# Split input weights kept in DRAM for later token tiles, and element work moved from GpSimd to VectorE

## The chip, the core and the metric

One core of one Trainium2 chip. The metric is the device time of one execution in microseconds (us); the lower, the better. Engines in the profile: PE is TensorE's matmul and PEld its weight load, DVE is VectorE, ACT is ScalarE, POOL is GpSimd, SP is SyncE, which here issues the DMAs.

## What is computed

One layer of a hybrid decoder block on x of 2048 tokens by 1024 features. `u = RMSNorm(x)`, then one projection `z = u @ W_in` whose columns feed two groups of heads: four mLSTM heads (columns for q, k, v, output gate and two gate columns per head) and four heads of differential attention (q, k, v). Both groups' outputs go through `W_out` and are added to x. After that come an MLP (`W_down (relu(norm @ W_up))^2`) and a gated per-layer embedding. All of it is float32 in the reference.

## The kernel before, in words

**Precision.** A float32 operand is split into two parts, hi and lo, and each product is three matmuls: hi by hi, hi by lo, lo by hi (`mm3`, lines 134 to 139; the three matmuls are lines 137, 138 and 139). The split itself is `split` (lines 74 to 76): ScalarE copies raw to hi (L75), and GpSimd, unless VectorE is named, subtracts hi from raw to give lo (L76).

**Two phases.** `phase1` (lines 176 to 594) makes the projection, both head groups and the first half of the output projection. `phase2` (from line 849) does the MLP and the rest; the change does not touch its code.

**Phase 1's projection.** The tokens are four tiles of 512 (j = 0 to 3). For each tile there is an attention pass ("a", 6 groups of 256 or 264 weight columns) and an mLSTM pass ("m", 8 groups of 256 columns), in the order a0, a1, a2, m0, m1, a3, m2, m3 (`ORDER`, line 37). So there are 4 times 14 = 56 group uses of 14 different groups. `load_w` (lines 242 to 256) loads one group as four pieces of 128 x 512 (128 x 528 for the group with the gate columns): a DMA from `w_in` into one of two raw buffers (L248), then `split` into one of eight slots of `wbuf`. `next_w` (line 265) is called when a group begins, and loads one group ahead of the one in use. As each group is used once per token tile, all 56 uses load and split their weights anew: 224 DMAs, 222 copies on ScalarE and 222 subtractions on GpSimd (two pieces of the very first group are split on VectorE alone, L251 and L252).

**The inputs.** `make_u` (line 313) runs at each change of token tile, eight times in all. `u_front` (lines 270 to 299) loads 128 tokens of x (L286), and the first time that a tile is seen it squares them on ScalarE (L291) and sums the eight feature blocks by three halving additions (L295), on VectorE for tile 0 and on GpSimd for the others; then VectorE multiplies by the norm's gain (L298). `u_back` (line 301) splits the result into hi and lo, the subtraction on VectorE, but on GpSimd for the odd blocks of tiles 1 to 3 (12 times in all), and makes the token's scale by a matmul with ones (L308) and a power on GpSimd (L310).

**Attention beside it.** `attention` (line 432) is a second generator that a credit counter interleaves with the projection (lines 572 to 593); it works on 64 units of 128 queries by one head. `attn_front` makes scores (L786, L789), their row maximum on VectorE (L790), the exponential on ScalarE (L798), and the difference of the two maps on VectorE (L810). `attn_back` transposes (L822), multiplies by V (L834), copies out (L837), makes the norm's factor (L840 to L842 and a power on GpSimd, L843) and scales the output by it on GpSimd (L844); a transposition on TensorE (L500) takes it from there. `qk_prep` (line 723) norms and rotates q and k on VectorE (L733, L736, L742 to L751) with a power on GpSimd between (L734), and `k_out` transposes them on TensorE (L758). `mlstm` runs one head's chunks in steps between the matmuls. The order of the instructions on each engine is set at build time by a scheduler that simulates the timeline, so it need not be that of the text.

Of the kernel before, what the change touches and what calls it, by code (L numbers as in the profile page):

```python
# [7 lines left out]
F32 = mybir.dt.float32  # L8
F32R = mybir.dt.float32r
BF16 = mybir.dt.bfloat16  # L10
AF = mybir.ActivationFunctionType
ALU = mybir.AluOpType
AX = mybir.AxisListType
# [3 lines left out]
P = 128  # L17
D = 1024
S = 2048
KT = D // P  # L20
# [19 lines left out]
@with_exitstack  # L40
def hybrid_block(ctx: ExitStack, tc: tile.TileContext, a: dict, out: bass.AP):
    nc = tc.nc

    const = ctx.enter_context(tc.tile_pool(name="const", bufs=1))
    dram = ctx.enter_context(tc.tile_pool(name="dram", bufs=1, space=DRAM))

    shared = ctx.enter_context(tc.tile_pool(name="shared", bufs=1))
    banks = Banks(ctx.enter_context(tc.tile_pool(name="banks", bufs=1, space=PSUM)))

    yT = [dram.tile([D, T2], F32, name=f"yT_d{i}") for i in range(NT2)]  # L50
    hd = dram.tile([D, T1], F32, name="h_d")
    qkdr = dram.tile([NH, NT1, P, 4, T1], F32, name="qk_d")
    vdr = dram.tile([NH // 2, NT1, P, 4, 2 * P], F32, name="v_d")

    wbuf = shared.tile([P, 2 * NW * 528], F32R, name="wbuf")
    ubuf = shared.tile([P, 16 * T1], F32R, name="ubuf")
    ybuf = shared.tile([P, 3 * 1024], F32R, name="ybuf")
    pre = shared.tile([P, T1], F32, name="pre")
    acc0 = shared.tile([P, T1], F32, name="acc0")
    rbuf = shared.tile([P, max(4096, 3072 + NR * 528)], F32, name="rbuf")  # L60

    ident = const.tile([P, P], F32, name="ident")
    identr = const.tile([P, P], F32R, name="identr")
    identb = const.tile([P, P], BF16, name="identb")
    masks = const.tile([P, 2, P], BF16, name="masksb")
    ones = const.tile([P, P], F32, name="ones")
    nc.vector.memset(ones, 1.0)
    negh = const.tile([P, 1], F32, name="negh")
    g23 = const.tile([P, 3, KT], F32, name="g23")
    nc.vector.memset(negh, -0.5)  # L70
    warm = const.tile([P, 1], F32, name="warm")
    nc.scalar.activation(warm, negh, AF.Copy)

    def split(raw, hi, lo, eng=nc.gpsimd):
        nc.scalar.activation(hi, raw, AF.Copy)  # L75
        eng.tensor_tensor(out=lo, in0=raw, in1=hi.bitcast(F32), op=ALU.subtract)  # L76

    nb = T1 // P

    def rstd_col(sq, pc, v):  # L80

        for b in range(nb):
            nc.tensor.matmul(pc[:, b:b + 1], lhsT=sq[:, b * P:(b + 1) * P], rhs=ones[:, 0:1], start=True, stop=True)
        nc.vector.tensor_scalar(out=v, in0=pc[:, 0:nb], scalar1=1.0 / D, scalar2=EPS, op0=ALU.mult, op1=ALU.add)
        nc.gpsimd.tensor_tensor(out=v, in0=v, in1=negh.broadcast_to([P, nb]), op=ALU.pow)

    def spread(v, pb, out_t):

        for b in range(nb):
            nc.vector.tensor_scalar(out=out_t[:, b * P:(b + 1) * P], in0=ident, scalar1=v[:, b:b + 1], scalar2=None,  # L90
                                    op0=ALU.mult)
        nc.tensor.matmul(pb, lhsT=ones, rhs=out_t, start=True, stop=True)
        nc.vector.tensor_copy(out_t, pb)

    phase1(tc, a, wbuf, ubuf, rbuf, banks, yT, hd, qkdr, vdr, ident, identr, identb, masks, ones, negh, split, rstd_col, spread, acc0)
    phase2(tc, a, wbuf, ubuf, rbuf, ybuf, pre, acc0, g23, banks, yT, hd, out, split, rstd_col, spread)


def cut(buf, base, *dims, cast=None):
    n = 1  # L100
    for d in dims:
        n *= d
    t = buf[:, base:base + n]
    if cast:
        t = t.bitcast(cast)
    if len(dims) == 2:
        t = t.rearrange("p (a b) -> p a b", a=dims[0])
    elif len(dims) == 3:
        t = t.rearrange("p (a b c) -> p a b c", a=dims[0], b=dims[1])
    return t  # L110
# [62 lines left out]
        return cut(t[0:shape[0]], 0, *shape[1:], cast=None if dtype == F32 else dtype)  # L173


def phase1(tc, a, wbuf, ubuf, rbuf, ps, yT, hd, qkdr, vdr, ident, identr, identb, masks, ones, negh, split, rstd_col, spread, acc0):
    nc = tc.nc
    with ExitStack() as ctx:
        pool = lambda name, bufs=1, **k: ctx.enter_context(tc.tile_pool(name=name, bufs=bufs, **k))
# [3 lines left out]
        pm = Ring(pool("p1m"))  # L183
        pc = pool("p1c")
        pw = Ring(None)
        half = NW * 528
        for tag, base in (("whi", 0), ("wlo", half)):
            pw.put(tag, [cut(wbuf, base + i * 528, 2, 264) for i in range(NW)])
        pu.put("xk", [cut(rbuf, i * 1024, KT, P) for i in range(2)])
        pu.put("sq", [cut(rbuf, 2048, KT, P)])  # L190
        pw.put("wraw", [cut(rbuf, 3072 + i * 528, 2, 264) for i in range(NR)])
# [47 lines left out]
        gB = gcol.unsqueeze(2).broadcast_to([P, KT, P])  # L239
        pl = lambda t: t.rearrange("p a b -> p (a b)")  # L240

        def load_w(g, width, first=False):
            r = []
            for k in range(0, KT, 2):
                raw = pw.tile([P, 2, 264], F32, tag="wraw")[:, :, :width]
                hi = pw.tile([P, 2, 264], F32R, tag="whi")
                lo = pw.tile([P, 2, 264], F32R, tag="wlo")
                nc.sync.dma_start(raw, w_in[g, :, k:k + 2, :width])  # L248
                hi, lo = hi[:, :, :width], lo[:, :, :width]
                if first and k % 4 == 0:  # L250
                    nc.vector.tensor_copy(hi, raw)  # L251
                    nc.vector.tensor_tensor(out=lo, in0=raw, in1=hi.bitcast(F32), op=ALU.subtract)  # L252
                else:
                    split(raw, hi, lo)
                r += [(hi[:, i], lo[:, i]) for i in range(2)]
            return r

        wseq, wq = [], []
        for kind, j in ORDER:
            if kind == "a":  # L260
                wseq += [(8, 264)] + [(8 + g, 256) for g in range(1, 6)]
            else:
                wseq += [(g, 256) for g in (0, 1, 2, 3, 4, 5, 7, 6)]

        def next_w():
            while wseq and len(wq) < 1 + AHEAD:
# [3 lines left out]
        def u_front(j, tb):  # L270
            if rcol[j] is None:
                rcol[j] = pc.tile([P, 2, 4], F32, name=f"rcol{j}")
                stats.add(j)
            xk = pu.tile([P, KT, P], F32, tag="xk", name="xk")
            start = j == 0 and tb == 0 and j in stats
            if start:
                for k in range(KT):
                    if k % 4 == 0:
                        nc.sync.dma_start(xk[:, k:k + 4], a["x_in"][0, :, k:k + 4])
                    if k == 0:  # L280
                        wq.append(load_w(*wseq.pop(0), True))
                    nc.scalar.activation(Uh[:, 0, k], xk[:, k], AF.Copy, scale=gcol[:, k:k + 1])
                    nc.vector.scalar_tensor_tensor(out=Ul[:, 0, k], in0=xk[:, k], scalar=gcol[:, k:k + 1],
                                                   in1=Uh[:, 0, k].bitcast(F32), op0=ALU.mult, op1=ALU.subtract)
            else:
                nc.sync.dma_start(xk, a["x_in"][4 * j + tb])  # L286
            acc = None
            if j in stats:
                sq = pu.tile([P, KT, P], F32, tag="sq", name="sq", bufs=1)
                acc = pu.tile([P, P], F32, tag="acc", name="acc", bufs=2)  # L290
                nc.scalar.activation(pl(sq), pl(xk), AF.Square)  # L291
                n = KT // 2
                while n:
                    o = sq[:, 0:n] if n > 1 else acc.unsqueeze(1)
                    (nc.gpsimd if j > 0 else nc.vector).tensor_tensor(out=o, in0=sq[:, 0:n], in1=sq[:, n:2 * n], op=ALU.add)  # L295
                    n //= 2
            if not start:
                nc.vector.tensor_tensor(out=xk, in0=xk, in1=gB, op=ALU.mult)  # L298
            return None if start else xk, acc

        def u_back(j, tb, xk, acc):
            if xk is not None:
                split(xk, Uh[:, tb], Ul[:, tb], nc.gpsimd if j and tb % 2 else nc.vector)
            if acc is not None:
                r = rcol[j]
                c = r[:, 0, tb:tb + 1]
                pr = ps.tile([P, 1], F32, "m")
                nc.tensor.matmul(pr, lhsT=acc, rhs=ones[:, 0:1], start=True, stop=True)  # L308
                nc.vector.tensor_scalar(out=c, in0=pr, scalar1=1.0 / D, scalar2=EPS, op0=ALU.mult, op1=ALU.add)
                nc.gpsimd.tensor_tensor(out=c, in0=c, in1=negh, op=ALU.pow)  # L310
                nc.vector.tensor_scalar(out=r[:, 1, tb:tb + 1], in0=c, scalar1=0.5, scalar2=None, op0=ALU.mult)
# [503 lines left out]
def attn_back(nc, pa, ps, st, i, h, front, VV, ident, negh, out):  # L815
# [25 lines left out]
    nc.vector.scalar_tensor_tensor(out=ss[:, 1:2], in0=ll[:, 0:1], scalar=EPS, in1=ll[:, 0:1], op0=ALU.mult, op1=ALU.mult)  # L841
    nc.vector.scalar_tensor_tensor(out=ss[:, 0:1], in0=ss[:, 0:1], scalar=1.0 / P, in1=ss[:, 1:2], op0=ALU.mult, op1=ALU.add)  # L842
    nc.gpsimd.tensor_tensor(out=ss[:, 0:1], in0=ss[:, 0:1], in1=negh, op=ALU.pow)  # L843
    nc.gpsimd.tensor_scalar(out=y, in0=y, scalar1=ss[:, 0:1], scalar2=None, op0=ALU.mult)  # L844
    out.append(y)
    yield 0.5

# [375 lines left out]
```

## Time and profile before

| | us |
|---|---|
| median of three runs | 3005.1 (3004.28 to 3007.91) |
| the profiled execution, its own time | 2999.47 |
| its span, first to last instruction | 2997.7 |
| TensorE matmul busy in the span | 2872.7 (96%) |
| VectorE, ScalarE, GpSimd busy | 1963.7, 1377.7, 1267.0 |
| mean granted TensorE clock | 0.988 |

Busy time is the union of an engine's instructions. A wait is put down to whoever released it last. Phase 1 fills the span up to some 1290 us and phase 2 the rest; the eight projection passes begin at about 6 (a0), 112 (a1), 242 (a2), 372 (m0), 525 (m1), 703 (a3), 839 (m2) and 1016 us (m3), and m3's last group ends at about 1220 us.

### The profile page before, as it was taken

How to read it: one execution, taken by the hardware profiler on the slowest of the kernel's cores; microseconds unless marked ns; L12 is line 12 of the kernel's file. 1: busy time of each engine (PE TensorE's matmuls, PEld its weight loads, DVE VectorE, ACT ScalarE, POOL GpSimd, SP SyncE). 2: the span in 40 equal slices, each digit the busy share in tenths (PEclk: the TensorE clock that was granted, in tenths of full speed). 3: DMA queues.
4: the chain of work that ended last, by engine and by line, in shares of the span. 5: the costliest groups of instructions: out<-in, count | busy, mean ns of one | idle time of the engine just before them, and what ended most of it. 6: DMA issues, size and time to landing. Idle time of an engine off the chain costs nothing.

```text
span 2997.7 us, 43151 instructions
## 1 busy us (share of the span) xinstructions
PE 2872.7 (96%) x15752; PEld 2460.7 (82%) x15752; DVE 1963.7 (66%) x3917; ACT 1377.7 (46%) x3134; POOL 1267.0 (42%) x980
## 2 busy tenths in 40 slices
PE   7798999899999899989999999999999999999999
PEld 7787988888988788867888888888878888888887
DVE  7788777767786766567555656564486555565653
ACT  4476766766666665544223332252342233322331
POOL 5666543434443332344333333362563333333441
PEclk9899999999999999999999999999999999999999
DMA  5654544334443423341111111124411111111211
GB/s 160 193 159 146 175 135 123 110 103 138 140 128 96 123 81 100 105 163 49 51 57 43 57 57 50 53 75 154 134 60 53 57 43 57 57 50 50 80 48 64
DMA packets 202421, 282.57 MB, mean 94 GB/s; under 512 B 16096, under 2 KB 143584, under 8 KB 198112
## 3 DMA queue, kind: packets, MB, share of 16 engines
q1 hardware_dynamic: 202208, 279.81, 30.7%
q8 instruction: 124, 2.03, 0.3%
q14 instruction: 89, 0.73, 0.1%
HBM read 239.90 MB, written 39.85 MB: 93 GB/s over the span
## 4 chain that ended last, share of the span: by engine, by line
PE 69%; DVE 14%; ACT 5%; DMA 4%; issue 4%; POOL 3%; SPq 0%; POOLq 0%; ACTq 0%; DVEq 0%
PE bank L923 52%; PE bank L137 3%; PE bank L138 3%; PE bank L139 3%; PE bank L834 2%; DMA rbuf<-in_w_in_dram 2%; DVE qn_r L736 2%; POOL wbuf L76 2%; DVE PP_r L810 2%; ACT PP_r L798 1%; DVE mxp_r L790 1%; PE bank L786 1%; PE bank L789 1%; PE bank L822 1%; POOL rn_r L734 1%
## 5 line engine op out<-in xcount | busy, mean ns | idle before, releaser
L76 POOL TENSOR_TENSOR wbuf<-rbuf,wbuf 128x512 fp32r<-128x512 f32 (+2 forms) x632 | 911.8, 1450 | 1321.8 <-ACT wbuf L75 1230.0
L75 ACT ACTIVATE wbuf<-rbuf 128x512 fp32r<-128x512 f32 (+2 forms) x632 | 415.1, 662 | 870.2 <-PE bank L923 600.7
L923 PE MATMUL bank<-U_r,wbuf 128*128 128x512 f32 x2928 | 701.1, 392 | 10.3 <-POOL wbuf L76 4.7
L923 PEld LDWEIGHTS bank<-U_r,wbuf 128*128 128x128 f32 x2928 | 551.1, 189 | 129.9 <-POOL wbuf L76 6.1
L923 PE MATMUL bank<-ubuf,wbuf 128*128 128x512 f32 x2208 | 574.7, 391 | 2.2 <-DVE ubuf L76 1.4
L888 DVE TENSOR_TENSOR h_r<-bank,h_r 128x512 f32<-128x512 f32 x504 | 343.3, 688 | 269.1 <-PE bank L923 267.5
L923 PEld LDWEIGHTS bank<-ubuf,wbuf 128*128 128x128 f32 x2208 | 414.8, 188 | 92.7 <-issue 2.9
L923 PE MATMUL bank<-ybuf,wbuf 128*128 128x512 f32 x1872 | 477.5, 390 | 5.4 <-ACT wbuf L75 4.6
L923 PEld LDWEIGHTS bank<-ybuf,wbuf 128*128 128x128 f32 x1872 | 351.3, 188 | 80.2 <-ACT wbuf L75 5.9
L137 PE MATMUL bank<-wbuf,ubuf 128*128 128x256 f32 (+1 forms) x1280 | 381.1, 298 | 25.0 <-ACT og_r L397 10.1
L138 PE MATMUL bank<-wbuf,ubuf 128*128 128x256 f32 (+1 forms) x1280 | 375.4, 293 | 0.9 <-DVE wbuf L252 0.9
L139 PE MATMUL bank<-wbuf,ubuf 128*128 128x256 f32 (+1 forms) x1280 | 373.6, 292 | 0.6 <-DVE ubuf L76 0.6
L137 PEld LDWEIGHTS bank<-wbuf,ubuf 128*128 128x128 f32 x1280 | 250.4, 196 | 34.1 <-ACT og_r L397 12.6
L138 PEld LDWEIGHTS bank<-wbuf,ubuf 128*128 128x128 f32 x1280 | 251.1, 196 | 3.9 <-DVE wbuf L252 1.5
L139 PEld LDWEIGHTS bank<-wbuf,ubuf 128*128 128x128 f32 x1280 | 250.5, 196 | 2.8 <-DVE ubuf L76 0.7
L790 DVE TENSOR_REDUCE mxp_r<-bank 128x1 f32<-128x512 f32 (+3 forms) x320 | 186.3, 603 | 68.6 <-PE bank L789 68.1
L798 ACT ACTIVATE PP_r<-bank,mx_r 128x512 f32<-128x512 f32 (+3 forms) x320 | 196.3, 622 | 53.8 <-DVE mx_r L795 47.4
L834 PE MATMUL bank<-V_r,at_r 128*128 128x128 f32 x1088 | 137.8, 279 | 0.9 <-ACT at_r L825 0.5
L786 PE MATMUL bank<-KT_r,QT_r 128*128 128x512 f32 (+3 forms) x320 | 124.7, 390 | 12.8 <-ACT PP_r L798 10.9
L834 PEld LDWEIGHTS bank<-V_r,at_r 128*128 128x128 f32 x1088 | 132.3, 196 | 3.4 <-ACT at_r L825 0.8
L137 PE MATMUL bank<-ubuf,wbuf 128*128 128x512 f32 x320 | 130.2, 407 | 2.4 <-DVE mx_r L794 1.2
L139 PE MATMUL bank<-ubuf,wbuf 128*128 128x512 f32 x320 | 127.8, 399 | 0.0
(285 smaller groups left out, 4244.8 us busy)
## 6 DMA issues: line engine op xcount, KB each, us to landing
rbuf<-in_w_in_dram SPq DMA_DIRECT2D x208, 256.0 KB, 2.8
rbuf<-in_w_down_dram SPq DMA_DIRECT2D x128, 256.0 KB, 2.6
rbuf<-in_w_up_dram SPq DMA_DIRECT2D x32, 1024.0 KB, 4.8
KT_r<-qk_d SPq DMA_DIRECT2D x40, 512.0 KB, 5.0
qk_d<-kst_r SPq DMA_DIRECT2D x64, 256.0 KB, 3.1
QT_r<-qk_d SPq DMA_DIRECT2D x128, 128.0 KB, 3.4
rbuf<-in_w_out_dram SPq DMA_DIRECT2D x32, 512.0 KB, 3.8
rbuf<-in_x_in_dram SPq DMA_DIRECT2D x31, 512.0 KB, 3.8
```

What stands on the lines that cost most here:

```text
L75: nc.scalar.activation(hi, raw, AF.Copy)
L76: eng.tensor_tensor(out=lo, in0=raw, in1=hi.bitcast(F32), op=ALU.subtract)
L137: nc.tensor.matmul(ps, lhsT=lh, rhs=rh, start=(start and i == 0), stop=False)
L138: nc.tensor.matmul(ps, lhsT=lh, rhs=rl, start=False, stop=False)
L139: nc.tensor.matmul(ps, lhsT=ll, rhs=rh, start=False, stop=(stop and i == n - 1))
L736: nc.vector.scalar_tensor_tensor(out=qn[:, e], in0=qn[:, e], scalar=rn[:, e:e + 1], in1=qkg[:, e // 2], op0=ALU.mult, op1=ALU.mult)
L786: nc.tensor.matmul(Sp[:, 0:n], lhsT=QT[:, 0, m], rhs=rhs, start=True, stop=False)
L790: nc.vector.tensor_reduce(out=mxp[:, m, ci:ci + 1], in_=Sp[:, 0:n], op=ALU.max, axis=AX.X)
L798: nc.scalar.activation(pp[:, 0:n], sps[ci][:, 0:n], AF.Exp, bias=mx[:, m:m + 1], scale=0.125, accum_out=lp[:, m, ci:ci + 1])
L834: nc.tensor.matmul(po, lhsT=ats[kb // 4][:, (kb % 4) * P:(kb % 4 + 1) * P], rhs=VV[kb // 4][:, kb % 4], start=(kb == 0), stop=(kb == i))
L888: eng.tensor_tensor(out=out, in0=x, in1=y, op=op)
L923: nc.tensor.matmul(p, lhsT=l, rhs=r, start=start and i == q == 0, stop=stop and i == n - 1 and q == 2, skip_group_check=on)
```

## The change

- `load_w` gets a flag `keep`. A group loaded with it is split as before, and each of its four split pieces (hi and lo, 512 KB) is then stored to a new DRAM tensor `wsd`, two loads later (`store_w`). Any later use of that group loads hi and lo straight from `wsd` into the slot: one DMA of 512 KB in place of one of 256 KB, a copy and a subtraction. The attention groups 3 to 5 are kept in a0, the groups 0 to 2 in a1, the mLSTM groups in m0.
- A slot of `wbuf` now holds hi and lo side by side; there are still eight.
- The sum of the eight squared blocks is one VectorE reduction over a permuted view, for all tiles.
- `u_back` subtracts on VectorE always.
- The scaling of an attention unit's output (L844) moves from GpSimd to VectorE.

```
+    wsd = dram.tile([14, KT // 2, P, 4, 264], F32, name="ws_d")
...
-        half = NW * 528
-        for tag, base in (("whi", 0), ("wlo", half)):
-            pw.put(tag, [cut(wbuf, base + i * 528, 2, 264) for i in range(NW)])
+        pw.put("ws", [cut(wbuf, i * 1056, 2, 2, 264) for i in range(NW)])
...
+        kept, late_st = set(), []
+        flat4 = lambda t: t.bitcast(F32).rearrange("p a b c -> p (a b) c")
+        def store_w(lag):
+            while len(late_st) > lag:
+                ws, g, k, n = late_st.pop(0)
+                nc.sync.dma_start(wsd[g, k // 2, :, :, :n], flat4(ws)[:, :, :n])
-        def load_w(g, width, first=False):
+        def load_w(g, width, keep, first=False):
             r = []
             for k in range(0, KT, 2):
+                ws = pw.tile([P, 2, 2, 264], F32R, tag="ws")
+                hi, lo = ws[:, 0, :, :width], ws[:, 1, :, :width]
+                if g in kept:
+                    store_w(0)
+                    nc.sync.dma_start(flat4(ws)[:, :, :width], wsd[g, k // 2, :, :, :width])
+                    r += [(hi[:, i], lo[:, i]) for i in range(2)]
+                    continue
                 raw = pw.tile([P, 2, 264], F32, tag="wraw")[:, :, :width]
...
+                if keep:
+                    late_st.append((ws, g, k, width))
+                store_w(2)
+            if keep:
+                kept.add(g)
             return r
...
-                wseq += [(8, 264)] + [(8 + g, 256) for g in range(1, 6)]
+                wseq += [(8 + g, 256 if g else 264, j == (0 if g >= 3 else 1)) for g in range(6)]
...
-                wseq += [(g, 256) for g in (0, 1, 2, 3, 4, 5, 7, 6)]
+                wseq += [(g, 256, j == 0) for g in (0, 1, 2, 3, 4, 5, 7, 6)]
...
-                n = KT // 2
-                while n:
-                    o = sq[:, 0:n] if n > 1 else acc.unsqueeze(1)
-                    (nc.gpsimd if j > 0 else nc.vector).tensor_tensor(out=o, in0=sq[:, 0:n], in1=sq[:, n:2 * n], op=ALU.add)
-                    n //= 2
+                nc.vector.tensor_reduce(out=acc, in_=sq.rearrange("p a b -> p b a"), op=ALU.add, axis=AX.X)
...
-                split(xk, Uh[:, tb], Ul[:, tb], nc.gpsimd if j and tb % 2 else nc.vector)
+                split(xk, Uh[:, tb], Ul[:, tb], nc.vector)
...
-    nc.gpsimd.tensor_scalar(out=y, in0=y, scalar1=ss[:, 0:1], scalar2=None, op0=ALU.mult)
+    nc.vector.tensor_scalar(out=y, in0=y, scalar1=ss[:, 0:1], scalar2=None, op0=ALU.mult)
```

## Rows read from the trace of the kernel before

**Rows 1.** Busy time in eight stretches, one for each projection pass (a0, a1, a2, m0, m1, a3, m2, m3), and their sum: from:to and length in us, then for each engine busy us and its instructions, the granted TensorE clock, the busy share of the DMA engines, and GB/s.

```profile
0.00:112.00 112.00, 87.45 (x646) 83.13 (x647) 83.17 (x247) 51.36 (x96) 63.87 (x56) 0.98 0.60 172
112.00:242.00 130.00, 115.58 (x870) 106.94 (x870) 112.31 (x406) 82.45 (x235) 84.14 (x82) 0.94 0.60 177
242.00:372.00 130.00, 117.98 (x925) 110.83 (x924) 104.52 (x329) 88.49 (x237) 76.00 (x74) 0.97 0.52 153
372.00:525.00 153.00, 148.46 (x1022) 133.09 (x1021) 120.75 (x301) 100.52 (x291) 64.65 (x55) 1.00 0.44 128
525.00:703.00 178.00, 168.63 (x1160) 151.73 (x1159) 128.72 (x314) 124.69 (x358) 74.68 (x64) 0.99 0.37 110
703.00:839.00 136.00, 125.99 (x984) 118.61 (x984) 100.23 (x307) 91.16 (x243) 65.44 (x63) 0.97 0.50 146
839.00:1016.00 177.00, 168.99 (x1123) 149.72 (x1123) 134.07 (x302) 115.52 (x321) 66.71 (x54) 0.98 0.36 103
1016.00:1220.00 204.00, 189.97 (x1285) 168.31 (x1283) 134.54 (x328) 130.15 (x373) 57.47 (x50) 0.98 0.33 95
sum 1220.00, PE 1123.05 PEld 1022.36 DVE 918.31 ACT 784.33 POOL 552.98; mean PE 140.38 PEld 127.80 DVE 114.79 ACT 98.04 POOL 69.12
```

**Rows 2.** Who TensorE waited for, up to 1290 us: the waiting instruction, what released it, us in total, times, the longest.

```profile
PE bank L758 <- DVE KS_r L751: 20.4, 13, 6.1
PE bank L786 <- ACT PP_r L798: 10.9, 14, 3.6
PE bank L137 <- ACT og_r L397: 10.1, 6, 3.6
...
PE bank L500 <- POOL ya_r L844: 3.4, 6, 0.9
...
PE bank L138 <- DVE wbuf L252: 0.9, 2, 0.5
```

**Rows 3.** The same kind of row as in the first group, for the instructions that write or read `wbuf` alone, from 0 to 1220 us.

```profile
0.00:1220.00 1220.00, 759.89 (x4608) 645.47 (x4608) 2.26 (x4) 141.11 (x224) 305.14 (x224) 0.98 0.44 130
```

**Rows 4.** The copy to hi (L75) up to 1220 us: what its engine's idle time before it waited for, and who waited for it (us, times).

```profile
  DMA rbuf<-in_w_in_dram: 94.3, 63
...
  POOL wbuf L76: 308.4, 100
```

**Rows 5.** Instructions in order of time in m3 (start us, us; in brackets the idle time before, and what ended it).

```profile
1131.36 0.63 ACT L75 ACTIVATE wbuf<-rbuf 128x512 fp32r<-128x512 f32 x1 [3.46 <-DMA rbuf<-in_w_in_dram]
...
1133.01 0.36 ACT L397 ACTIVATE og_r<-bank,rcol 128x128 f32<-128x128 f32 x1
...
1133.42 0.39 PE L137 MATMUL bank<-wbuf,ubuf 128*128 128x256 f32 x1 [3.58 <-ACT og_r L397]
```

**Rows 6.** VectorE's instructions up to 1300 us, shapes apart: count, busy us, mean ns of one, idle before them.

```profile
L790 DVE TENSOR_REDUCE mxp_r<-bank 128x1 f32<-128x512 f32 x224 | 149.1, 683 | 49.5 <-PE bank L789 49.5
L810 DVE SCALAR_TENSOR_TENSOR PP_r<-PP_r,sc_r 128x512 f32<-128x512 f32 x112 | 95.2, 893 | 0.9
L736 DVE SCALAR_TENSOR_TENSOR qn_r<-qn_r,rn_r,qkg 128x64 f32<-128x64 f32 x256 | 92.0, 415 | 14.7 <-POOL rn_r L734 14.2
L413 DVE SCALAR_TENSOR_TENSOR cv_r<-zc_r,cw,cv_r 128x512 f32<-128x512 f32 x96 | 91.3, 951 | 12.3 <-ACT cv_r L411 11.6
...
L76 DVE TENSOR_TENSOR ubuf<-rbuf,ubuf 128x1024 fp32r<-128x1024 f32 x19 | 25.1, 1324 | 2.2 <-ACT ubuf L75 2.1
```

**Rows 7.** Single lines of the program on VectorE: count, duration in ns as min/median/max; the second row is what L736 waited for (us, times).

```profile
L736 DVE SCALAR_TENSOR_TENSOR qn_r<-qn_r,rn_r,qkg x256: 247/277/2408, 43.8 to 853.1; 128x64 f32<-128x64 f32 x128
...
  POOL rn_r L734: 14.2, 19
...
L413 DVE SCALAR_TENSOR_TENSOR cv_r<-zc_r,cw,cv_r x96: 734/752/2870, 404.5 to 1219.2; 128x512 f32<-128x512 f32 x96
...
L810 DVE SCALAR_TENSOR_TENSOR PP_r<-PP_r,sc_r x160: 339/746/2896, 126.7 to 1240.4; 128x512 f32<-128x512 f32 x112, 128x128 f32<-128x128 f32 x16, 128x256 f32<-128x256 f32 x16, 128x384 f32<-128x384 f32 x16
...
L90 DVE TENSOR_SCALAR row_r<-ident,rcol x16: 272/282/1241, 21.1 to 991.9; 128x128 f32<-128x128 f32 x16
```

**Rows 8.** One GpSimd row (two subtractions) and one VectorE row (a copy of 128 x 3) from the timeline of m0.

```profile
407.24 2.59 POOL L76 TENSOR_TENSOR wbuf<-rbuf,wbuf 128x512 fp32r<-128x512 f32 x2 [2.14 <-ACT wbuf L75]
...
407.25 1.30 DVE L408 COPY zc_r<-tail 128x3 f32<-128x3 f32 x1
```

**Rows 9.** GpSimd's instructions up to 1300 us, shapes apart, as in the sixth group.

```profile
L844 POOL TENSOR_SCALAR ya_r<-ya_r,ass_r 128x128 f32<-128x128 f32 x64 | 47.2, 737 | 5.3
L843 POOL TENSOR_TENSOR ass_r<-ass_r,negh 128x1 f32<-128x1 f32 x64 | 39.6, 618 | 153.0 <-DVE ass_r L842 130.3 <-DVE mx_r L794 11.8 <-ACT Dm_r L678 7.5
L76 POOL TENSOR_TENSOR ubuf<-rbuf,ubuf 128x1024 fp32r<-128x1024 f32 x12 | 29.5, 2462 | 20.0 <-ACT ubuf L75 20.0
```

**Rows 10.** The DMA queue that SP feeds (packets, MB, share of the span of 16 engines), issues by line (count, KB each, median us from issue to landing), and the landing times of the weight loads (L248).

```profile
q1 hardware_dynamic: 202208, 279.81, 30.7%
...
rbuf<-in_w_in_dram SPq DMA_DIRECT2D x208, 256.0 KB, 2.8
...
KT_r<-qk_d SPq DMA_DIRECT2D x40, 512.0 KB, 5.0
qk_d<-kst_r SPq DMA_DIRECT2D x64, 256.0 KB, 3.1
...
DMA to landing us min/median/max: 2.5/2.8/9.2
```

More of the change, by code (lines that the diff above doesn't have):

```diff
@@ L93, in spread @@
         nc.vector.tensor_copy(out_t, pb)
-    phase1(tc, a, wbuf, ubuf, rbuf, banks, yT, hd, qkdr, vdr, ident, identr, identb, masks, ones, negh, split, rstd_col, spread, acc0)
+    phase1(tc, a, wbuf, ubuf, rbuf, banks, yT, hd, qkdr, vdr, wsd, ident, identr, identb, masks, ones, negh, split, rstd_col, spread, acc0)
     phase2(tc, a, wbuf, ubuf, rbuf, ybuf, pre, acc0, g23, banks, yT, hd, out, split, rstd_col, spread)
@@ L173, in tile, with phase1 @@
         return cut(t[0:shape[0]], 0, *shape[1:], cast=None if dtype == F32 else dtype)
-def phase1(tc, a, wbuf, ubuf, rbuf, ps, yT, hd, qkdr, vdr, ident, identr, identb, masks, ones, negh, split, rstd_col, spread, acc0):
+def phase1(tc, a, wbuf, ubuf, rbuf, ps, yT, hd, qkdr, vdr, wsd, ident, identr, identb, masks, ones, negh, split, rstd_col, spread, acc0):
     nc = tc.nc
@@ L240, in phase1 @@
         pl = lambda t: t.rearrange("p a b -> p (a b)")
-        def load_w(g, width, first=False):
+        kept, late_st = set(), []
[5 more added lines that the diff above has]
+        def load_w(g, width, keep, first=False):
             r = []
             for k in range(0, KT, 2):
+                ws = pw.tile([P, 2, 2, 264], F32R, tag="ws")
[5 more added lines that the diff above has]
+                    continue
                 raw = pw.tile([P, 2, 264], F32, tag="wraw")[:, :, :width]
-                hi = pw.tile([P, 2, 264], F32R, tag="whi")
-                lo = pw.tile([P, 2, 264], F32R, tag="wlo")
                 nc.sync.dma_start(raw, w_in[g, :, k:k + 2, :width])
-                hi, lo = hi[:, :, :width], lo[:, :, :width]
                 if first and k % 4 == 0:
```

## Prediction, made before the change was run

> **What bounds the kernel now.** I first cut phase 1 into its eight projection passes [rows 1]. From a1 to m3, 112 to 1220 us, TensorE is idle for 14.4, 12.0, 4.5, 9.4, 10.0, 8.0 and 14.0 us (length less PE), 72.4 us together, and its granted clock lies under 1.00: length times what is missing gives 7.8, 3.9, 0, 1.8, 4.1, 3.5 and 4.1, 25.2 us. So about 98 us of visible loss can be won there at all; phase 2's code is not touched. No other engine is full: VectorE comes nearest, 112 of 130 us in a1 and 104 of 130 in a2; ScalarE has 784 of 1220 us.
>
> Second, who ended TensorE's waits [rows 2]: VectorE's k parts (L751) 20.4 us, ScalarE's exponentials (L798) 10.9 and its gate (L397) 10.1, the scaled attention output (L844) 3.4. The input weights, which this change is about, hardly appear: 0.9 us. TensorE does not wait for weights. What it waits for is work that stands in the same queues as their splitting.
>
> That work is large [rows 3]: 224 copies in 141.1 us of ScalarE (0.63 each) and 224 subtractions in 305.1 us of GpSimd (1.36 each), the first two of `W_out` among them. Worse than its length is what it does in a queue: ScalarE sat idle 94.3 us before copies whose raw weights had not landed, 63 times [rows 4]. One case shows the price [rows 5]: at 1131.36 a copy had waited 3.46 us for its DMA; the gate behind it (L397) began at 1133.01, and TensorE lost 3.58 us to it.
>
> On VectorE the same subtractions show as stretched instructions. L790, with its one operand in PSUM, takes 683 ns on average; L736, L413 and L810, which read two tiles of SBUF, average 415, 951 and 893 [rows 6], against medians of 277, 752 and 746 and maxima over 2400 [rows 7]. A copy of three columns lasted 1.30 us beside two subtractions on GpSimd [rows 8]. Mean less median times count: 256 x 0.138 + 96 x 0.199 + 112 x 0.147 = 35.3 + 19.1 + 16.5 = 71 us of VectorE.
>
> **What the change removes.** Of 56 group uses, a1 takes 3 from DRAM, a2 and a3 6 each, m1, m2 and m3 8 each: 39, so 156 of 224 pieces. It does what it says: the flags make each group kept at its first or second use, and everything later finds it.
> - ScalarE: 156 x 0.63 = 98 us of copies, and 156/224 of the 94.3 us of waits, 66 us: 164 of 878 us, 19%.
> - GpSimd: 156 x 1.36 = 212 us, L844's 47.2 and the x splits' 29.5 [rows 9], 289 of 553 us, 52%, besides the sums of squares.
> - VectorE gets back about 52% of the 71 us of stretch: 37 us.
>
> **What it adds to VectorE.** Twelve new reductions over 1024 elements (tile 0's four replace additions already on VectorE and count as even). No such view is in the trace: the half-size L790 at 0.68 us is a floor, GpSimd's 2.46 us for a 128 x 1024 subtraction [rows 9] a ceiling; I take twice L790, 1.37, as it is the same operation: 16 us. Twelve x splits at 1.32 us [rows 6]: 16 us. The 64 scalings between 0.27 and 1.24 us, as L90 of the same shape [rows 7]; at its median of 0.28, 18 us. Together 50 us, against 37 returned: VectorE's total hardly moves, but the passes m1 to m3 gain (few additions there) and a1 gains nothing.
>
> [...]
>
> **A new wait on VectorE.** L844 now stands in VectorE's queue and waits for GpSimd's power (L843); behind it stand row maxima and differences of the next unit, for which ScalarE's exponentials and then TensorE's score banks wait. The nearest row is L736, which also waits for a power, 64 times: 14.2 us in 19 waits [rows 7]. Ends: below nothing, minus 3.4, as TensorE's wait for L844 is shorter when the scaling takes 0.28 and not 0.74 us; above, all 64 powers in full, 39.6 us [rows 9]. I take 14.2, with half on the path: 7 us.
>
> **The DMAs.** A kept load lands in between 2.8 us (the 256 KB piece) and 5.0 us (512 KB, KT) [rows 10]; I take 5.0, against 2.8 + 0.63 + 1.36 = 4.8 today. It is issued a group ahead, and a group lasts 19 to 22 us (112/6 in a0, 130/6 in a1, 153/8 in m0), which hides either. If that cover went, all 156 would be exposed. On SP it waits for the last matmul on its slot, with attention's loads queued behind it; those are issued ahead too, and today the queue waits for GpSimd's release of the raw buffers at the same place. Nothing. The 56 stores follow two pieces behind, when the raw buffer's reuse has already waited for the same subtraction; the flush ahead of the first kept load waits for two splits, twice in the program. A store takes 0.524 MB of DMA time, by the queue's 30.7% of 2997.7 us for 279.81 MB 3.29 us a MB, so 1.7 us; it lands at most in twice the 3.1 us of the 256 KB store. In a0, a1 and m0 it lies beside raw loads: four of them need (2.8 + 0.63 + 1.36) x 4 / 2 = 9.6 us in two buffers, within 19 us. Nothing, with the cover named; the other case is the rival below.
>
> **The sum.** ScalarE-ended waits, 21.0 us: half, 10.5 (ends: the 19% of load, 4, and all, 21). Half, because the waits for raw weights, the longest thing in that queue, go wholly. L844's 3.4: all. L751's 20.4: a quarter, 5 (0 to 20); the power before it comes free and L736 is less stretched, but a0 and half of a1 stay. The other 72.4 - 44.8 = 27.6 us: a quarter, 7 (0 to 14). That is 26. Clock: each gap closed takes its share of the 25.2 us, 25.2 x 26/72.4 = 9. Less 7 for the new wait: 28 us. The profiled execution, 2999.5 us (span 2997.7), would become 2971.5; it lies 0.19% under the median of the runs, and from that median, 3005.1, I forecast **2977 us**. The terms' ends do not fall together; this case's own range is 2960 to 2995.
>
> **Rivals.**
> - *More room than the idle time shows.* TensorE loads weights in 939 of the seven passes' 1108 us [rows 1], 169 us without, not 72. For: a matmul row is as long as its pipeline, so short stalls vanish into busy time. Against: matmuls of 512 columns leave weight loading idle without any stall. If stalls fill the 169 us at the same shares, 28 x 169/72.4 = 65 us: 2940. [...] 13%.
> - *Nothing.* Weights were never waited for (0.9 us), a wait that closes is opened by the next late producer, VectorE, which is no lighter in the a passes: 3005, within 6 us. 13%. I count under 0.2%, 6 us, as no change: a measurement of this kernel can tell no less.
> - *Slower: the stores make the raw weights late* in a0's second half, a1 and m0. The DMA share rises in a1 by (12 x 0.524 + 12 x 0.262) x 3.29 = 31 us, from 0.60 to 0.84, in m0 by 32 x 1.72 = 55 us, from 0.44 to 0.80. It decides when a landing takes over 7.5 us: then four pieces, (7.5 + 2.0) x 2 = 19 us, outlast m0's group. At the 9.2 us that today's slowest landing took [rows 10], a group needs 22.4 us: 3.3 late in eight groups of m0, 3.7 in three of a0, 0.7 in six of a1, 42 us; with half of the gain kept, 3005 + 42 - 14 = 3033. Against: today's median is 2.8. 12%.
>
> **How the numbers follow.** Forecast 62%, more room 13%, nothing 13%, slower 12%. Faster by over 0.2%: 75%; within: 13%; slower: 12%. The range 2944 to 3010 holds the forecast, nothing, and the nearer half of the larger gain; it leaves out the slower case and the rest.
>
> **What would show it.** Right: copies to hi and subtractions into `wbuf` fall to 68 up to 1220 us; ScalarE's waits for raw weights fall to about 30 us; L736 and L413 come near their medians; TensorE's waits for L798 and L397 halve; m1, a3, m2 and m3 get shorter by 3 to 8 us each, a0 and m0 stay. Wrong: TensorE waiting on `wbuf` or SP on stores in m0 (the slower rival); VectorE idle before L844 for more than 14 us; the same waits as before under other names (nothing); passes shorter by more than their idle time (more room).

## The result

| | before | after |
|---|---|---|
| median, us | 3006.25 (4 runs) | 2961.3 (2951.68 to 2962.63, 4 runs) |
| ratio of the two | | 0.9842, 95% interval 0.9829 to 0.9855 |
| the profiled execution, us | 2999.47 | 2962.63 |
| its mean granted clock | 0.988 | 0.982 |

The change is faster by 45 us of median; 28 were forecast. (The quotient of the two medians is 0.985, inside the ratio's interval.) The two profiled executions are 36.8 us apart: the one of after is the slowest of its four, the one of before lay under its median. Where these 37 us lie is read from the two traces.

The profile after by projection pass, same columns as [rows 1]:

```profile
0.00:107.00 107.00, 85.20 (x645) 80.53 (x646) 87.25 (x241) 48.39 (x92) 48.36 (x46) 0.97 0.74 227
107.00:235.00 128.00, 115.90 (x889) 109.49 (x888) 107.74 (x439) 80.26 (x230) 44.33 (x45) 0.92 0.88 277
235.00:356.00 121.00, 113.56 (x906) 108.39 (x905) 91.54 (x332) 77.27 (x209) 31.37 (x35) 0.97 0.72 222
356.00:505.00 149.00, 148.41 (x1018) 133.67 (x1018) 108.02 (x303) 98.34 (x287) 49.31 (x40) 0.99 0.77 238
505.00:692.00 187.00, 177.33 (x1194) 156.83 (x1193) 124.89 (x340) 111.24 (x335) 9.39 (x13) 0.96 0.49 152
692.00:814.00 122.00, 119.56 (x957) 114.89 (x956) 88.36 (x316) 78.03 (x211) 23.80 (x26) 0.97 0.70 212
814.00:997.00 183.00, 175.72 (x1183) 156.42 (x1181) 121.73 (x325) 105.84 (x309) 10.69 (x12) 0.98 0.51 159
997.00:1185.00 188.00, 179.13 (x1218) 160.93 (x1216) 115.02 (x316) 107.27 (x322) 14.02 (x14) 0.97 0.42 128
sum 1185.00, PE 1114.81 PEld 1021.15 DVE 844.55 ACT 706.64 POOL 231.26; mean PE 139.35 PEld 127.64 DVE 105.57 ACT 88.33 POOL 28.91
```

The passes end 35 us earlier; what lies behind them gives the other 2. a0 gives 5. In a1 to m3 TensorE's idle time (length less PE) falls from 72.4 to 48.4, 24 us, and its busy time by 6 (1035.6 to 1029.6). Their weight loading stays at 939 and 941 us, so the time without a weight load falls from 169 to 137: by that count all 30 us of these passes are regained gaps. Single passes compare badly: a3 lost 27 of its 984 matmul rows while m1 gained 34 on 1160; attention work changed places.

Who TensorE waited for, up to 1258 us, as in [rows 2], and one more row of before:

```profile
PE bank L771 <- DVE KS_r L764: 7.8, 7, 2.1
PE bank L138 <- ACT ubuf L76: 7.2, 3, 2.8
PE bank L513 <- DVE ya_r L857: 6.7, 4, 2.9
...
PE bank L799 <- DMA KT_r<-qk_d: 3.9, 1, 3.9
...
PE bank L799 <- ACT PP_r L811: 3.2, 6, 1.1
...
PE bank L138 <- ACT og_r L410: 2.1, 4, 0.7
PE bank L139 <- POOL wbuf L77: 2.1, 2, 1.6
```
```profile
PE bank L137 <- ACT ubuf L75: 3.2, 2, 3.0
```

The numbers of lines have moved, by 13 here and by 1 in `split` and `mm3`: L771, L799, L513, L138 and L76 are L758, L786, L500, L137 and L75 of before. The three largest waits of before have shrunk (20.4 to 7.8, 10.9 to 3.2, 10.1 to 2.1). Smaller ones grew: the waits for the attention output (3.4 to 6.7) and for ScalarE's copy of the inputs (3.2 to 7.2) doubled. All of TensorE's waits in this view add to 98.9 us before and 73.4 after.

The instructions on `wbuf` up to 1185 us ([rows 3]), and what ScalarE's copy to hi waited for ([rows 4]):

```profile
0.00:1185.00 1185.00, 750.75 (x4608) 642.97 (x4608) 3.30 (x4) 44.76 (x69) 95.91 (x69) 0.97 0.63 194
```
```profile
  DMA rbuf<-in_w_in_dram: 37.6, 22
```

VectorE, shapes apart ([rows 6]), and the scaling that moved to it (min/median/max):

```profile
L823 DVE SCALAR_TENSOR_TENSOR PP_r<-PP_r,sc_r 128x512 f32<-128x512 f32 x112 | 81.0, 765 | 1.0
L426 DVE SCALAR_TENSOR_TENSOR cv_r<-zc_r,cw,cv_r 128x512 f32<-128x512 f32 x96 | 73.1, 762 | 8.3 <-ACT cv_r L424 7.7
L749 DVE SCALAR_TENSOR_TENSOR qn_r<-qn_r,rn_r,qkg 128x64 f32<-128x64 f32 x256 | 63.0, 300 | 13.7 <-POOL rn_r L747 13.5
...
L77 DVE TENSOR_TENSOR ubuf<-rbuf,ubuf 128x1024 fp32r<-128x1024 f32 x31 | 38.0, 1226 | 5.1 <-ACT ubuf L76 5.1
L309 DVE TENSOR_REDUCE acc_r<-rbuf 128x128 f32<-128x1024 f32 x16 | 31.2, 1953 | 4.0 <-ACT rbuf L308 4.0
```
```profile
L857 DVE TENSOR_SCALAR ya_r<-ya_r,ass_r x64: 264/281/1299, 129.0 to 1254.9; 128x128 f32<-128x128 f32 x64
...
  POOL ass_r L856: 4.4, 9
```

The first three are the multiplies of [rows 6] that averaged 893, 951 and 415 ns. The queue that SP feeds ([rows 10]):

```profile
q1 hardware_dynamic: 268128, 350.20, 38.0%
...
wbuf<-ws_d SPq DMA_DIRECT2D x148, 512.0 KB, 5.6
...
ws_d<-wbuf SPq DMA_DIRECT2D x52, 512.0 KB, 5.1
KT_r<-qk_d SPq DMA_DIRECT2D x40, 512.0 KB, 5.9
qk_d<-kst_r SPq DMA_DIRECT2D x64, 256.0 KB, 4.8
...
rbuf<-in_w_in_dram SPq DMA_DIRECT2D x60, 256.0 KB, 3.9
```

70 MB more, and the transfers that [rows 10] has too land later (KT 5.0, the store of q and k 3.1, the raw weights 2.8 us before); TensorE waited 3.9 us for one of attention's loads (1.8 before), but for no kept weight.

### The profile page after: what moved, and what is told of

Read it like the earlier page. It is cut to its first block, busy times and chain, and to the rows that moved or that the text cites. A ratio compares the mean times of both kernels' runs of the same rounds, so it can differ in the third digit from the quotient of the medians.

```text
span 2960.8 us, 42686 instructions
## 1 busy us (share of the span) xinstructions
PE 2866.7 (97%) x15752; PEld 2465.1 (83%) x15752; DVE 1888.7 (64%) x3997; ACT 1300.3 (44%) x2978; POOL 943.0 (32%) x712
## 4 chain that ended last, share of the span: by engine, by line
PE 82%; DVE 9%; DMA 4%; ACT 2%; issue 1%; POOL 1%; SPq 0%; ACTq 0%; DVEq 0%; POOLq 0%
PE bank L936 52%; PE bank L138 6%; PE bank L139 6%; PE bank L140 6%; PE bank L847 4%; PE bank L802 2%; PE bank L799 2%; PE bank L835 2%; DMA rbuf<-in_x_in_dram 2%; DMA rbuf<-in_w_in_dram 1%; DVE acc_r L309 1%; DVE ubuf L77 1%; DVE mxp_r L803 1%; ACT PP_r L811 1%; DVE qn_r L749 1%
## 5 line engine op out<-in xcount | busy, mean ns | idle before, releaser
L77 POOL TENSOR_TENSOR wbuf<-rbuf,wbuf 128x512 fp32r<-128x512 f32 (+2 forms) x476 | 702.7, 1481 | 1099.0 <-ACT wbuf L76 1021.5
L76 ACT ACTIVATE wbuf<-rbuf 128x512 fp32r<-128x512 f32 (+2 forms) x476 | 317.9, 670 | 807.8 <-PE bank L936 597.3
L936 PE MATMUL bank<-ubuf,wbuf 128*128 128x512 f32 x2208 | 575.3, 391 | 1.2 <-ACT ubuf L76 0.8
L138 PE MATMUL bank<-wbuf,ubuf 128*128 128x256 f32 (+1 forms) x1280 | 378.2, 296 | 18.1 <-ACT ubuf L299 5.9
L138 PEld LDWEIGHTS bank<-wbuf,ubuf 128*128 128x128 f32 x1280 | 249.6, 195 | 23.1 <-ACT ubuf L299 5.8
L856 POOL TENSOR_TENSOR ass_r<-ass_r,negh 128x1 f32<-128x1 f32 x64 | 39.5, 617 | 549.4 <-DVE ass_r L855 493.6
L799 PE MATMUL bank<-KT_r,QT_r 128*128 128x512 f32 (+3 forms) x320 | 125.7, 393 | 7.1 <-DMA KT_r<-qk_d 3.9
L138 PE MATMUL bank<-ubuf,wbuf 128*128 128x512 f32 x320 | 129.0, 403 | 3.7 <-ACT ubuf L76 2.6
```

Source lines behind the costliest of these rows:

```text
L138: nc.tensor.matmul(ps, lhsT=lh, rhs=rh, start=(start and i == 0), stop=False)
L799: nc.tensor.matmul(Sp[:, 0:n], lhsT=QT[:, 0, m], rhs=rhs, start=True, stop=False)
L936: nc.tensor.matmul(p, lhsT=l, rhs=r, start=start and i == q == 0, stop=stop and i == n - 1 and q == 2, skip_group_check=on)
```

## The experiments

Ratios are to the kernel before, run on the same chip, with 95% intervals. The scheduler rebuilds each engine's order for every edit, so each experiment also carries another order; four kernels below, each built in a second order, price that.

**Kept weights alone.** The changed kernel with the three element moves undone:

```
-                nc.vector.tensor_reduce(out=acc, ...)
+                (the three halving additions, on GpSimd for j > 0)
-                split(xk, Uh[:, tb], Ul[:, tb], nc.vector)
+                split(xk, Uh[:, tb], Ul[:, tb], nc.gpsimd if j and tb % 2 else nc.vector)
-    nc.vector.tensor_scalar(out=y, ...)
+    nc.gpsimd.tensor_scalar(out=y, ...)
```

> The kept weights alone; sums of squares, x splits and the attention output's scaling stay as before. Theory (the gain of 45 us comes from the work that kept weights take off ScalarE and GpSimd): 2961 to 2972 us, a ratio to the kernel before of 0.985 to 0.989; copies to wbuf fall from 224 to 68, ScalarE's waits for raw weights from 94 to about 38 us; the waits of TensorE for og_r and PP_r fall as in the changed kernel (10.1 and 10.9 to about 2 and 3), and the sums of squares on GpSimd cost little. Rival (half or more comes from the three moves to VectorE): 2980 to 2995 us.

**The moves alone**, the reverse: the kernel before with these three lines as after.

> The three moves to VectorE alone; all 56 group uses load and split their weights as before. Theory (gain from kept weights): no gain or a small loss, 3000 to 3015 us, because VectorE gets about 16 x 1.95 + 12 x 1.32 + 64 x 0.31 = 67 us of work and nothing back from the subtractions; only TensorE's 3.4 us behind the scaling can go. Rival (the moves carry half): 2980 to 2990 us.

Measured: 2958.52 us, 0.9847 (0.9834 to 0.986), and 3000.11 us, 0.9983 (0.9975 to 0.9992). The kept weights carry the whole gain; the moves bring 5 us alone, no more than another order can, and nothing beside them. Busy time up to phase 2's first output-projection matmul, columns as in [rows 1], of before, after, kept weights alone and, for later, the first burden below:

```profile
0.00:1285.00 1285.00, 1184.66 (x8352) 1073.46 (x8353) 944.32 (x2581) 815.86 (x2221) 579.53 (x509) 0.98 0.44 130
```
```profile
0.00:1249.00 1249.00, 1175.13 (x8319) 1071.85 (x8320) 870.44 (x2660) 737.39 (x2062) 255.33 (x242) 0.97 0.61 190
```
```profile
0.00:1238.00 1238.00, 1172.66 (x8351) 1069.40 (x8352) 853.23 (x2582) 740.77 (x2065) 374.09 (x355) 0.98 0.62 192
```
```profile
0.00:1287.00 1287.00, 1187.06 (x8344) 1075.64 (x8345) 941.34 (x2661) 735.15 (x2063) 438.14 (x400) 0.97 0.60 185
```

With the same VectorE work to do, the kept weights shorten VectorE's busy time by 91 us (944 to 853). The prediction gave it 37. The moves give VectorE time back as well, which neither the prediction nor the expectation saw: alone they bring it some 65 us of work (reductions 31, scalings 24, splits 15 more, additions 6 less), and its busy time rises by 15 (944 to 959), as GpSimd works 114 us less beside it (580 to 466).

**Another order of the same work.** The constant that paces attention against the projection, in four kernels:

```
-PACE = 0.85
+PACE = 0.86
```

> The changed kernel with the constant that paces attention against the projection at 0.86 in place of 0.85: the same instructions, interleaved otherwise. It measures what the order of instructions alone is worth. Expected within 6 us of the changed kernel, 2955 to 2967; if it lies further off, differences of that size between other variants show nothing about their edits.

> The kernel before with the pacing constant at 0.86: the same instructions in another order. Expected 2993 to 3018 us, within 13 of 3005; beside the changed kernel at 0.86 (2948) it gives the change's gain for a second order, which the theory puts at 35 to 60 us.

**Three contiguous additions on VectorE** in the changed kernel, in place of the permuted reduction, in both orders:

```
-                nc.vector.tensor_reduce(out=acc, in_=sq.rearrange("p a b -> p b a"), op=ALU.add, axis=AX.X)
+                n = KT // 2
+                while n:
+                    o = sq[:, 0:n] if n > 1 else acc.unsqueeze(1)
+                    nc.vector.tensor_tensor(out=o, in0=sq[:, 0:n], in1=sq[:, n:2 * n], op=ALU.add)
+                    n //= 2
```

> The changed kernel with the sum of squares as three halving additions over contiguous blocks, all on VectorE, in place of the one reduction over the permuted view. The reduction took 1.95 us, 16 times, 31 us in all. By half-size rows the additions should take about 0.6 + 0.35 + 0.25 = 1.2 us. Theory (at changes of token tile VectorE is the late producer): 12 us less VectorE work at the tile changes, 2 to 6 us faster than the changed kernel, 2955 to 2960. Rival (it is hidden): 2960 to 2963.

> The same other interleaving (0.86) for the version with three contiguous additions on VectorE in place of the reduction, which gave 2941 us at 0.85, 20 us below the changed kernel, where 2 to 6 us had been expected. Theory (the reduction itself costs 20 us at the changes of token tile): again 15 to 25 us under its partner of the same batch. Rival (most of the 20 us was a lucky order): 0 to 10 us under it.

**The stores alone.** The kernel of kept weights in which no kept copy is loaded, in both orders:

```
-                if g in kept:
+                if False and g in kept:
```

> The kernel of kept weights alone, but no kept copy is ever loaded: every use loads raw weights and splits them as before, and the 56 stores of 512 KB are made besides. It prices the stores. Theory (stores are hidden beside other transfers): 3003 to 3010 us, within 0.15% of before. Rival (the stores make the raw weights late in a0, a1 and m0): 3015 to 3045 us, with ScalarE's waits for raw weights up by 10 us or more there and TensorE waiting for wbuf.

> The stores without use (3019 us at 0.85, 13 above before) at 0.86. Theory (stores cost nothing that can be measured, the 13 us were the order): within 10 us of the kernel before at 0.86, on either side. Rival (stores cost 13 us): 10 to 20 us above it.

| | order at 0.85: us, ratio | at 0.86: us, ratio |
|---|---|---|
| before | 3006.25, 1 | 3009.86, 1.0019 (1.0009 to 1.0029) |
| changed | 2961.3, 0.9842 (0.9829 to 0.9855) | 2948.18, 0.9816 (0.9803 to 0.983) |
| changed, additions | 2941.24, 0.979 (0.9776 to 0.9804) | 2953.89, 0.9834 (0.982 to 0.9848) |
| stores without use | 3019.34, 1.0047 (1.0035 to 1.0059) | 3015.11, 1.0036 (1.0024 to 1.0049) |

Order alone moves a kernel by 4 to 13 us (3 to 13 by the ratios), more than the intervals leave open and up to twice the 6 us that I counted as no change. The additions look 20 us better in one order (16 by the ratios, which compare on one chip) and 6 worse in the other: the expected 2 to 6 us can be neither shown nor excluded, and most of the 20 was order (VectorE's busy time up to phase 2 is only 4 us shorter, 867 against 870). Their version at 0.85 is still the fastest that ran, 2941. The kernels with stores are slower by 13 us in one order and by 5 in the other (3015.11 against 3009.86), but not where the stores are made. All of them lie in a0, a1 and m0, the last at 485 us. Up to the end of m0, before and with the stores:

```profile
0.00:524.70 524.70, 469.17 (x3457) 433.69 (x3457) 420.46 (x1280) 322.52 (x853) 288.67 (x265) 0.97 0.53 156
```
```profile
0.00:522.80 522.80, 473.31 (x3445) 437.65 (x3445) 412.62 (x1271) 320.67 (x848) 292.49 (x266) 0.96 0.70 211
```

m0 ends 2 us earlier with the stores at nearly the same count of matmuls, and 3 us earlier in the other order (525.2 against 527.9); a1 is 8 us longer in both orders, a0 6 and 8 shorter. ScalarE's waits for raw weights up to there are 45.2 us, 56.6 without stores; the rival wanted 10 us more. What is lost comes behind the last store, where both kernels run the same instructions. So a cost of the stores is not shown. The change's own gain is 45 us in one order and 62 in the other (35 to 60 expected), and VectorE's busy time up to phase 2 falls alike in both (944 to 870, 946 to 876).

**What the kept weights relieve.** Four kernels put one burden back into the changed one, for each of the 156 kept pieces, on one of the raw buffers, which the kept pieces leave idle:

```
                     nc.sync.dma_start(flat4(ws)[:, :, :width], wsd[g, k // 2, :, :, :width])
+                    d = pw.tile([P, 2, 264], F32, tag="wraw")[:, :, :width]
+                    nc.gpsimd.tensor_tensor(out=d, in0=d, in1=d, op=ALU.subtract)   # 1
+                    nc.scalar.activation(d, d, AF.Copy)                             # 2
+                    nc.sync.dma_start(d, w_in[g, :, k:k + 2, :width])               # 3, ahead of the copy of 2
+                    nc.gpsimd.memset(d, 0.0)                                        # 4
```

> The changed kernel with a GpSimd subtraction of 128 x 512 put back for each of the 156 kept pieces, on an idle raw buffer: no copy, no DMA, nobody waits for it. It gives GpSimd back 156 x 1.36 = 212 us. Theory P (what the kept weights win is mostly VectorE's instructions that no longer stretch beside these subtractions): 20 to 40 of the 45 us are lost, 2980 to 3000 us, and the 64-column multiply of qk_prep goes back from 300 to about 390 ns on average. Theory S (it is ScalarE's queue, its copies and its waits for raw weights): 2960 to 2968 us. Order of instructions alone may move either by up to 10 us, as the two runs of the same batch with another interleaving will show.

> The changed kernel with a ScalarE copy of 128 x 512 put back for each of the 156 kept pieces, on an idle raw buffer: no DMA to wait for and no subtraction. It gives ScalarE back 156 x 0.63 = 98 us, but not the 57 us of waits for raw weights that went. Theory S in its form 'busy time': 2975 to 2990 us. Theory S in its form 'waits for raw weights' and theory P: 2960 to 2968 us.

> The changed kernel with, for each of the 156 kept pieces, the raw load and ScalarE's copy of it put back on the raw buffer, nothing on GpSimd. Beside the copies alone (2975 us) it brings back ScalarE's waits for raw weights. Theory of the prediction (the waits in that queue are the larger part): 2985 us or more, with ScalarE's waits for raw weights back near 94 us. Rival (VectorE's stretch is the larger part): 2965 to 2982 us, as without the loads.

> The changed kernel with a GpSimd memset of 128 x 512 in place of the subtraction that cost 33 us when it was put back for each of the 156 kept pieces. A memset reads nothing from SBUF, but occupies GpSimd's queue. Theory (the subtraction's two SBUF reads hold up VectorE's instructions with two SBUF operands): VectorE's total stays near the changed kernel's 1032 us up to the end of phase 1 (1107 with the subtractions), the 64-column multiply near 300 ns, and the time within an order's worth of the changed kernel, 2948 to 2972 us. Rival (GpSimd's queue: powers wait behind the dummy): 2980 us or more.

| put back | us, ratio | lost of the gain, us | VectorE, ScalarE, GpSimd busy to phase 2 |
|---|---|---|---|
| 1: subtraction | 2994.37, 0.9968 (0.9955 to 0.9981) | 33 | 941, 735, 438 |
| 2: copy | 2974.86, 0.9901 (0.9886 to 0.9916) | 14 | 877, 814, 266 |
| 3: raw load and copy | 3005.83, 1.0003 (0.9994 to 1.0012) | 45 | 880, 815, 259 |
| 4: memset | 2982.32, 0.9929 (0.9916 to 0.9942) | 21 | 895, 740, 332 |

These losses are differences of medians; by the ratios, which compare on one chip, they are 38, 18, 48 and 26 us. Theory P is borne out by the first: with subtractions that nobody waits for, VectorE works 71 us longer (870 to 941), and the powers are not later (VectorE waited 10.4 us for `rn_r` and 5.5 for `ass_r`, 13.5 and 4.4 in the changed kernel). The 64-column multiply went from 300 to 340 ns, though, not to 390. For theory S the second shows little: 14 us are hardly more than order alone moved, and they lie behind m3, which ends at 1184 us (1185 in the changed kernel) but leaves 402 matmul rows of phase 1 in place of 325. With the raw loads the loss is 45 us, clear of the order. ScalarE's waits are back too (what the third kernel's added copy waited for):

```profile
  DMA rbuf<-in_w_in_dram: 90.1, 70
```

The first and the third loss add to far more than the gain, so such prices are not shares of it. Two limits: nothing ties these burdens to a group, so 95 of the 156 subtractions, 93 copies and 78 loads fell into m1 (m1 lasts 193, 194 and 213 us, 186 in the changed kernel). For the subtractions that matters little: a1 and m0, which hold the other 61, are 10 and 9 us longer, m1 only 7. And the third burden goes beyond what the change took away: it adds 41 MB to the changed kernel's transfers (DMA share 0.97 in a1), and with the 39.5 us of the copies that were left ScalarE's waits for raw weights are 130 us, 94 before. Waits and contention are not told apart in it, and how much of the 45 us ScalarE's relief is worth stays open.

The memset met neither account: its time is the rival's, but the 64-column multiply stayed at 302 ns and the powers were no later, as the theory had it. (The expectation's 1032 and 1107 us of VectorE are no busy times up to phase 2; those are 870 and 941, and 895 here.) Its 156 memsets ran in long bunches, and during three of them, one in m0 and two in m1, VectorE stood still (GpSimd's and VectorE's timeline for the second, then TensorE's longest waits from 484 to 560 us):

```profile
526.62 11.28 POOL L259 MEMSET rbuf<- 128x512 f32 x24
```
```profile
530.34 7.64 DVE L859 TENSOR_SCALAR ya_r<-ya_r,ass_r 128x128 f32<-128x128 f32 x1
530.54 7.43 DVE L805 TENSOR_REDUCE mxp_r<-bank 128x1 f32<-128x512 f32 x1
```
```profile
PE bank L515 <- DVE mxp_r L805: 8.2, 1, 8.2
PE bank L700 <- DVE Dm_r L694: 6.0, 1, 6.0
PE bank L731 <- DVE og_r L724: 5.2, 1, 5.2
```

All seven VectorE rows begun between 530.3 and 532.8 us end at 537.97 or 537.98, as the memsets do (526.62 + 11.28 = 537.90). The three stalls last 7.8, 7.6 and 4.4 us, and TensorE waited 19.4 us behind them, most of the 21 us lost. So here it was not a late power on GpSimd's queue that cost, but VectorE's standing still beside the memsets. The subtractions' 71 us are another thing: no VectorE row up to phase 2 lasts over 3 us in that kernel.

## Why the prediction was right, and where its sum was not

**What bounds the kernel: right.** Weights were never waited for, and the gain came from what their splitting does to other work. The waits named as its source fell: ScalarE's two by 15.7 us (10.5 forecast, ends 4 to 21), KS by 12.6 (5, ends 0 to 20). Idle time in a1 to m3 fell by 24; forecast were 26 less 7 for the new wait, 19. How these 24 divide between ScalarE's queue and VectorE's stretch the burdens do not settle.

**What it removes: right in count** (69 copies where 68 were expected; waits for raw weights 37.6 where about 30 were), **wrong in VectorE's share, and this is the step that failed.** "VectorE gets back about 52% of the 71 us of stretch: 37 us" became 91 with the kept weights alone. I had counted mean less median on three lines. These gave back 48 of the 91 (busy 92.0 to 71.2, 91.3 to 74.7 and 95.2 to 84.3 us), so the share of 52% was low; the other 43 come from lines that I had left out. One is the 128 x 1 update of `sc_r` ahead of the difference of the maps: 305 ns on average before, 226 after, 321 with the first burden. So "VectorE's total hardly moves" was wrong: it fell by 74 us, with the new work on it. The first burden above shows what that is worth: 71 us of it back costs 33.

**What it adds.** The reduction took 1.95 us (1.37 taken, bounds 0.68 to 2.46). The splits took 1.23 us, the scaling 0.28 in the median, as forecast. TensorE's waits behind the sum of squares went from 0.7 to 2.6 us; beyond that the reduction's price is not seen in the time, as order moves more.

**The new wait: smaller, and elsewhere.** VectorE waited 4.4 us for the power, not 14.2. But TensorE's 3.4 us behind the scaling, which I let go wholly, became 6.7, since the scaling now stands behind the tile's element work, as in the longest of its four waits (start of m1, changed kernel; the power was ready at 519.6):

```profile
519.92 1.87 DVE L309 TENSOR_REDUCE acc_r<-rbuf 128x128 f32<-128x1024 f32 x1
521.71 1.22 DVE L311 TENSOR_TENSOR rbuf<-rbuf,gcol 128x1024 f32<-128x1024 f32 x1
...
523.58 0.28 DVE L857 TENSOR_SCALAR ya_r<-ya_r,ass_r 128x128 f32<-128x128 f32 x1
...
524.01 0.45 PE L513 MATMUL bank<-ident,ya_r 128*128 128x128 f32 x1 [2.94 <-DVE ya_r L857]
```

**The DMAs.** A kept load took 5.6 us, within its group's time, as forecast. "Nothing" for the stores stood, as far as is shown: the kernels with stores are no later up to the end of m0. The slower rival had the traffic right (DMA share 0.88 in a1 and 0.77 in m0, 0.84 and 0.80 reckoned), but raw loads landed in 3.9 us in the median, far from the 7.5 at which it decides.

**The clock: wrong in sign.** Length times what is missing of 1.00 went from 25.2 to 36 us (10.2, 3.6, 1.5, 7.5, 3.7, 3.7, 5.6 by pass), where 9 were to be won. Part of it is this execution: it had the lowest clock of the four runs, and the one at 0.990 took 2951.68.

**The sum.** Profiled execution against profiled execution 2971.5 was forecast, 2962.6 came: idle time 24 (19), clock and matmul rows together 6 (9), a0 5 (0), behind m3 2. That the sum came within 9 us is in part luck: VectorE's share was far too low, the clock had the wrong sign, and a0 was not expected to move. The passes show it: 3 to 8 us less each were forecast for m1, a3, m2 and m3, but m1 and m2 got 9 and 6 us longer and a3 and m3 14 and 16 shorter. A forecast to 10 us was not to be had here, as order alone moves that much.

**The rivals.** "More room" was right as a count, as all that a1 to m3 gained is time without a weight load; but it filled 31 of those 169 us, not 65. What it argued from is in the trace of before: matmul rows of 0.28 us begin 0.12 us apart (m0, at 461 us), and beside the 2928 rows of 512 columns on `U_r` in phase 2 (392 ns each, their weight loads 189) weight loading is idle for 129.9 us, the matmuls for 10.3. That time without a weight load is the count to go by finds weak support here: 7 of these 31 us had not shown as idle time of the matmuls. "Nothing" fell: some closed waits were opened again under other names (the inputs' copy, the attention output), but TensorE's waits fell by a quarter in all.

## What to carry to other kernels

Work that no one waits for had a price here, in what it did to the queues and to the neighbour engine (33 us for the subtractions put back): add up the stretch over all instructions of that neighbour, not over the three longest lines. A move that takes work off one engine can relieve the engine that it goes to: here some 65 us of work made VectorE's busy time only 15 us longer. A burden put back into the faster kernel prices it, but two such prices need not add up to the gain, and what nothing ties in place is bunched by the scheduler. Where a scheduler orders the program, build each variant in a second order before trusting a difference of ten microseconds.

## What the runs showed of the hardware

- VectorE stood still for up to 7.8 us while GpSimd ran 29, 24 and 17 memsets back to back. The first row that stood is a copy of three columns in the first stall and a `tensor_scalar` of 128 x 128 in the other two, and in the second the reduction and the multiply ahead of it took 1.98 and 1.22 us beside the same memsets (1.94 and 1.28 on average in this kernel). The rows waited for many memsets, not for one: to the end of the first two runs, and in the third to a gap of 0.06 us ahead of its last two. It need not be so: in the longest run, 43 memsets from 503.5 us, the same `tensor_scalar` took 0.62 us. Why, no run shows.
- GpSimd's subtractions, which read and write a raw buffer, cost VectorE more than its memsets, which only write it: up to phase 2 VectorE's busy time is 71 us longer with the subtractions and 25 with the memsets, of which the three stalls are some 20. The 64-column multiply says the same, not strongly: 340 ns with the subtractions, 302 with the memsets, 300 with neither, but 326 with the copies of the second burden, where only the order differs for VectorE. A subtraction of 128 x 512 also lasts longer (1.17 us, a memset 0.53), so no run shows that it is the reads.
- Landing times rose together with the traffic: at a share of 0.61 of the DMA engines up to phase 2, against 0.44, the 256 KB store of q and k took 4.8 us and not 3.1.
